# Partial sums and the residual added by accumulating transfers, PSUM copied by ACT

## The chip, the cores and the metric

The kernel runs on one core of a Trainium2 chip. A core has five engines that each work through their own instructions in order: PE (TensorE, matmuls, whose weight loads the profile lists as PEld), DVE (VectorE), ACT (ScalarE), POOL (GpSimd) and SP (SyncE, which here only starts transfers). They meet through semaphores. Matmuls write into PSUM, which DVE and ACT read; everything else lies in the core's buffer memory (SBUF) or in DRAM. Transfers (DMA) between DRAM and SBUF run beside the engines, on 16 DMA engines. The metric is the device time of one execution in microseconds (us). Before the change it is 1700.47 us, the median of three runs (1698.03 to 1700.65).

## The reference

One layer of a hybrid decoder for 2048 tokens of width 1024, in float32:

```python
h = rmsnorm(x, norm_pre)
proj = h @ w_in                       # 6416 columns, split into seven parts
y_ssd = ...                           # Mamba-2 scan of 16 heads, gated and normalised
y_sc = sc_b * causal_dwconv(sc_c * sc_h, sc_conv_w) * silu(z_sc)
mix = concatenate([y_ssd, y_sc]) @ w_out      # 2048 -> 1024
x = x + rmsnorm(mix, norm_post)               # the residual
gate = sigmoid(x @ w_ple_gate)                # 1024 -> 1024
return x + gate * (p @ w_ple_proj)
```

The change touches the second half of `mix`, its norm and the addition of the residual.

## The kernel before

All activations are held transposed: 128 of the 1024 features on the partitions, tokens along the free dimension. A tile is 128 x 512 float32, 256 KB; the 2048 tokens make four token groups (`tg` 0 to 3, `TG` = 512), the 1024 features eight blocks (`d` 0 to 7, `KD` = 8). Each float32 operand is split into a high part, a cast to the matmul's type, and the rest; a product takes three passes of matmuls (`PASSES`, function `mm3`). An output tile with eight input blocks thus takes 24 matmuls (line 214).

The program has four stages: the input projection with the convolutions (to about 1038 us), the scan of the heads, under which the half of `mix` that comes from `y_sc` is computed (tiles `os`, line 826, stored into DRAM as `part_d`), then the output projection's other half (`out_proj`, from about 1322 us), then the gate (`gate`, from about 1505 us).

In `out_proj` two token groups share the weights. A PSUM tile `mo` holds two output blocks, `d` and `d + 1`, of one group; three such tiles rotate (`pss`). For each block, in the order (group t, d), (t, d+1), (t+1, d), (t+1, d+1), PE does the 24 matmuls; then DVE adds the half in PSUM to the stored partial sum and writes the result as a tile of `x2` (line 1060), ACT squares it (lines 1062 and 1065), and DVE sums the squares into `ssq` (line 1066). `Loads` brings two blocks of `part_d`, 512 KB, per transfer into one of three buffers (line 769, on SP's queue). Below, the first block of a PSUM tile is its first half, the other its second half, and a unit is one block of one group: units 0 to 15 are groups 0 and 1, 16 to 31 groups 2 and 3, 32 to 63 the gate.

Other work is fixed to units by a table (`plan`): `mixes` prepares the operands `act_m` of a later group from loads `mraw` (lines 785, 203, 204); `norm` multiplies `ssq` with a matrix of 1/1024 on PE (`pn`, line 1072), takes the root on ACT and the reciprocal on DVE; `residual` scales `x2` on DVE (line 1081) and adds the input `x` to it (line 1082), loaded two blocks at a time as `xres` like `part`; `operands` makes the gate's operands `act_x2s` from it. Weights are loaded by SP, then cast by ACT (`ws_o`, line 138) and subtracted by DVE (line 139) into one of six slots.

The order in the source is not the order on the engines: a scheduler places the instructions of each engine by the times that it expects, within the dependencies, and every engine then runs its list in order. A waiting instruction holds up everything behind it on its engine, transfers on a queue too.

Of the kernel before, what the change touches and what calls it, by code (L numbers as in the profile page):

```python
# [7 lines left out]
F32 = mybir.dt.float32  # L8
F32R = mybir.dt.float32r
AF = mybir.ActivationFunctionType  # L10
ALU = mybir.AluOpType
# [4 lines left out]
P = 128  # L16
D = 1024
T = 2048
KD = D // P
KM = 2 * KD  # L20
TB = 1024
NB = T // TB
TG = 512
NG = T // TG
# [36 lines left out]
def hybrid_kernel(ctx: ExitStack, tc: tile.TileContext, xT, pT, w_t, w_dt, w_o, w_g, w_p, cols_d, cst_d, outT):  # L61
    nc = tc.nc
    V, S, G, TE = nc.vector, nc.scalar, nc.gpsimd, nc.tensor
# [7 lines left out]
    yz_d = [dram.tile([KD, P, TB], F32, name=f"yz_d{b}") for b in range(NB)]  # L71
# [4 lines left out]
    part_d = [dram.tile([KD, P, TG], F32, name=f"part_d{g}") for g in range(NG)]  # L76
    ysc_d = [dram.tile([KD, P, TB], F32, name=f"ysc_d{b}") for b in range(NB)]
# [262 lines left out]
    for b, prs, order in groups:  # L340
        src = lambda pr, i, jj, kk: w_t[tiles[pr][i], :, 4 * jj:4 * jj + 4, :]
# [20 lines left out]
    with ExitStack() as st:  # L362
# [352 lines left out]
        for b, prs, order in groups:  # L715
            to = {pr: takes(b, pr) for pr in prs}
            n = order_.index(prs)
# [28 lines left out]
    class Loads:  # L746
# [5 lines left out]
        def begin(self, kind, *at):  # L752
            if (kind, *at) in self.ready:
                return
            t = self.ready[(kind, *at)] = self.pool.tile([P, 2, TG], F32, tag="ld", name="_".join(map(str, (kind, *at))))
            if kind in ("mraw", "gn"):
                b, o = divmod(at[0] * TG, TB)
            if kind == "gn":
                src = grs_d[b][:, o:o + TG].partition_broadcast(P)
            else:  # L760
                if kind == "mraw":
                    k = at[1]
                    src = yz_d[b][k:k + 2, :, o:o + TG] if k < KD else ysc_d[b][k - KD:k - KD + 2, :, o:o + TG]
                elif kind == "part":
                    src = part_d[at[0]][at[1]:at[1] + 2]
                else:
                    src = xT[at[1]:at[1] + 2, :, at[0] * TG:(at[0] + 1) * TG]
                src = src.rearrange("k p t -> p k t")
            nc.sync.dma_start(t, src)

# [21 lines left out]
    def mm_bank(name):  # L792
        return psm.tile([P, TG], F32, tag="mm", name=name)
# [241 lines left out]

    with ExitStack() as st:
        pp = st.enter_context(tc.tile_pool(name="pp", bufs=2))
        L3 = Loads(st, "pl3", 3)

        x2s_, ssq_, rs_, sp_ = {}, {}, {}, {}  # L1040

        def out_proj(t):

            for tg in (t, t + 1):
                x2s_[tg] = [None] * KD
                ssq_[tg] = pp.tile([P, TG], F32, tag="ssq", name=f"ssq2_{tg}")
            for dp in range(0, KD, 2):
                sp = []
                for tg in (t, t + 1):
                    x2, ssq = x2s_[tg], ssq_[tg]  # L1050
                    ps = pss.tile([P, 2, TG], F32, tag="ssd", name=f"mo_{tg}_{dp}")
                    pt = L3.get("part", tg, dp)
                    for i in range(2):
                        for q in range(2):
                            if tg == t:
                                sp.append(W.next(len(sp)))
                            mm3([(ps[:, i, :], sp[2 * i + q], acts_o[tg])], 4 * q, 4, KD)
                        d = dp + i
                        x2[d] = pp.tile([P, TG], F32, tag="x2", name=f"x2_{tg}_{d}", bufs=NG * KD)
                        V.tensor_tensor(x2[d], ps[:, i, :], pt[:, i, :], ALU.add)  # L1060
                        if d == 0:
                            S.activation(ssq, x2[d], AF.Square)
                        else:
                            sq = pp.tile([P, TG], F32, tag="sq2", name=f"sq2_{tg}_{d}")
                            S.activation(sq, x2[d], AF.Square)
                            V.tensor_tensor(ssq, ssq, sq, ALU.add)
                        yield

        def norm(tg):

            ps = mm_bank(f"pn2_{tg}")
            TE.matmul(ps, ones_d, ssq_[tg], start=True, stop=True)
            rs = rs_[tg] = pp.tile([P, TG], F32, tag="rs2", name=f"rs2_{tg}")
            S.activation(rs, ps, AF.Sqrt, bias=epsc[:, 0:1])
            V.reciprocal(rs, rs)

        def residual(tg, d):

            x2, xk = x2s_[tg], L3.get("xres", tg, d)
            for i in range(2):  # L1080
                V.scalar_tensor_tensor(x2[d + i], x2[d + i], col(C_POST + d + i), rs_[tg], ALU.mult, ALU.mult)
                V.tensor_tensor(x2[d + i], x2[d + i], xk[:, i, :], ALU.add)

        def operands(tg, d):

# [27 lines left out]
        def after(unit, *steps):  # L1113
            plan.setdefault(unit, []).extend(steps)

        def second(tg, at_norm, at_res, at_ops):

            after(at_norm, lambda: norm(tg))
            for n, u in enumerate(at_res):
                after(u - 1, lambda d=2 * n: L3.begin("xres", tg, d))  # L1120
                after(u, lambda d=2 * n: residual(tg, d))
            for n, u in enumerate(at_ops):
                after(u, lambda d=2 * n: operands(tg, d))
# [15 lines left out]
        u = 0  # L1139
# [68 lines left out]
```

## Time and profile before

| What | Value |
|---|---|
| Median of three runs | 1700.47 us (1698.03 to 1700.65) |
| The profiled execution | 1696.41 us, its span 1694.7 us |
| Busy in the span | PE 98%, PEld 80%, DVE 74%, ACT 46%, POOL 3% |
| Chain that ended last | PE 85%, DMA 6%, DVE 6%, ACT 2%, issue 1% |
| Output projection, `mo` (line 214) | 768 matmuls, 180.9 us busy, 4.3 us idle before them |
| Gate, `mg` (line 214) | 768 matmuls, 176.8 us busy, 0.7 us idle before them |
| TensorE clock granted | 0.996 of full speed |

A row of a group reads: line, engine, operation, output and inputs with shapes, count, then busy time and the mean ns of one, then the idle time of the engine just before them and what ended it. In the rows of waits the engine and line on the left waited for what is on the right: us in total, times, longest. A row of the chain of waits or of the timeline begins with its start and its length in us. A row of windows holds the stretch, its length, the busy time of PE, PEld, DVE, ACT and POOL with their instructions, the granted clock, the DMA engines' busy share, and GB/s. A row of DMA issues ends with the count, the KB of one and the median us from issue to landing.

### The profile page before, as it was taken

The page shows a single profiled execution, that of the slowest core. Times are in us where ns is not written, and L with a number is a line of the kernel's source. Part 1 is how long each engine was busy: PE and PEld are TensorE (multiplying, and loading weights), DVE is VectorE, ACT ScalarE, POOL GpSimd, SP SyncE. Part 2 cuts the span into 40 slices and gives each one's busy share as a digit, 9 for nine tenths or more (in the row PEclk, how much of TensorE's full clock was granted, in tenths as well). Part 3 has the DMA queues.
Part 4 walks back from the last instruction along what each step waited for, and adds up shares of the span by engine and source line. Part 5 has one row for each costly group of instructions (what it writes and reads, how often), then busy time and mean ns, then how long its engine had stood idle before and what let it go on. Part 6 is the DMA issues. An engine that isn't in the chain of part 4 may idle for free.

```text
span 1694.7 us, 22635 instructions
## 1 busy us (share of the span) xinstructions
PE 1658.7 (98%) x8324; PEld 1351.9 (80%) x8324; DVE 1255.4 (74%) x1843; ACT 783.5 (46%) x1408; POOL 45.6 (3%) x79
## 2 busy tenths in 40 slices
PE   7999999999999999999999999999999899999998
PEld 5788888888888888888888888778777677788886
DVE  7997777988669867677777685689678748878632
ACT  7763444434337434343444353666575324252421
POOL 0000000000000100100000000000000000000000
PEclk9999999999999999999999999999999999999999
DMA  9462221773226322222222237789887735636422
GB/s 303 162 211 70 97 96 61 257 251 120 69 68 213 130 80 95 78 76 68 106 82 102 73 117 239 245 277 278 261 314 242 243 100 168 197 102 211 149 95 87
DMA packets 122691, 262.27 MB, mean 155 GB/s; under 512 B 17098, under 2 KB 19658, under 8 KB 121556
## 3 DMA queue, kind: packets, MB, share of 16 engines
q1 hardware_dynamic: 122580, 260.83, 46.4%
q8 instruction: 65, 1.06, 0.2%
q14 instruction: 46, 0.38, 0.1%
HBM read 192.45 MB, written 68.33 MB: 154 GB/s over the span
## 4 chain that ended last, share of the span: by engine, by line
PE 85%; DMA 6%; DVE 6%; ACT 2%; issue 1%; SPq 0%; DVEq 0%; ACTq 0%
PE mg L214 10%; PE mo L214 8%; PE os L826 6%; PE py L967 1%; PE A_xs1X L310 1%; PE A_gc6X L310 1%; PE A_gc7X L310 1%; PE A_gb6X L310 1%; PE A_z3X L310 1%; PE A_xs3X L310 1%; PE A_gc5X L310 1%; PE A_z2X L310 1%; PE A_xs2X L310 1%; PE A_gb4X L310 1%; PE A_gc4X L310 1%; PE A_gc3X L310 1%
## 5 line engine op out<-in xcount | busy, mean ns | idle before, releaser
L826 PE MATMUL os<-act_m,ws_os 128*128 128x512 f32 x768 | 186.0, 396 | 2.4 <-ACT po L830 1.7
L214 PE MATMUL mo<-act_m,ws_o 128*128 128x512 f32 x768 | 180.9, 396 | 4.3 <-DVE x L1060 4.3
L214 PEld LDWEIGHTS mo<-act_m,ws_o 128*128 128x128 f32 x768 | 144.1, 189 | 42.1 <-issue 6.1
L214 PE MATMUL mg<-act_x2s,ws_g 128*128 128x512 f32 x768 | 176.8, 391 | 0.7 <-ACT gth L1104 0.7
L826 PEld LDWEIGHTS os<-act_m,ws_os 128*128 128x128 f32 x768 | 141.2, 188 | 37.6 <-issue 6.6
L214 PEld LDWEIGHTS mg<-act_x2s,ws_g 128*128 128x128 f32 x768 | 143.0, 188 | 34.2 <-ACT gth L1104 4.4
L139 DVE TENSOR_TENSOR ws_A_gb<-wr_A_gb,ws_A_gb 128x512 fp32r<-128x512 f32 x96 | 65.8, 686 | 33.0 <-ACT ws_A_gb L138 32.9
L138 ACT CAST ws_A_gc<-wr_A_gc 128x512 fp32r<-128x512 f32 x96 | 59.7, 622 | 57.7 <-PE A_gc5X L310 8.3
L138 ACT CAST ws_A_gb<-wr_A_gb 128x512 fp32r<-128x512 f32 x96 | 59.7, 621 | 51.6 <-PE A_cb0Y L310 4.3
L604 DVE SCALAR_TENSOR_TENSOR xo<-ux,cols,xo 128x1024 f32<-128x1024 f32 x60 | 76.7, 1280 | 6.7 <-ACT xo L600 5.6
L939 ACT ACTIVATE m<-m,adt 128x128 f32<-128x128 f32 x256 | 77.5, 391 | 0.6 <-DMA m<-acs_d 0.5
L139 DVE TENSOR_TENSOR ws_A_gc<-wr_A_gc,ws_A_gc 128x512 fp32r<-128x512 f32 x96 | 66.0, 687 | 14.1 <-ACT ws_A_gc L138 12.8
L1105 DVE SCALAR_TENSOR_TENSOR gth<-gth,pe 128x512 f32<-128x512 f32 x32 | 22.1, 691 | 70.5 <-ACT gth L1104 70.4
L1104 ACT ACTIVATE gth<-mg 128x512 f32<-128x512 f32 x32 | 19.1, 598 | 103.7 <-PE mg L214 103.6
L214 PE MATMUL A_ple<-act_p,ws_p 128*128 128x512 f32 x192 | 48.2, 409 | 9.0 <-ACT ws_p L138 8.1
L942 DVE SCALAR_TENSOR_TENSOR m<-m,gsb 128x1024 f32<-128x1024 f32 x32 | 39.6, 1246 | 19.1 <-ACT m L939 16.8
L214 PEld LDWEIGHTS A_ple<-act_p,ws_p 128*128 128x128 f32 x192 | 37.4, 196 | 18.7 <-ACT ws_p L138 9.0
L139 DVE TENSOR_TENSOR ws_A_z<-wr_A_z,ws_A_z 128x512 fp32r<-128x512 f32 x48 | 32.9, 685 | 25.2 <-ACT ws_A_z L138 25.2
L203 ACT CAST act_m<-mraw 128x512 fp32r<-128x512 f32 x64 | 38.1, 621 | 28.9 <-DVE mraw L785 15.8
L138 ACT CAST ws_A_xs<-wr_A_xs 128x512 fp32r<-128x512 f32 x48 | 29.9, 623 | 44.3 <-issue 11.6
L138 ACT CAST ws_A_z<-wr_A_z 128x512 fp32r<-128x512 f32 x48 | 29.9, 623 | 41.9 <-DVE wr_A_z L187 8.6
L1060 DVE TENSOR_TENSOR x<-mo,part 128x512 f32<-128x512 f32 x32 | 22.0, 686 | 29.3 <-PE mo L214 29.3
(499 smaller groups left out, 3597.7 us busy)
## 6 DMA issues: line engine op xcount, KB each, us to landing
wr_A_gc<-in_w_t_dram SPq DMA_DIRECT2D x64, 256.0 KB, 2.5
wr_A_gb<-in_w_t_dram SPq DMA_DIRECT2D x64, 256.0 KB, 2.8
m<-acs_d SPq DMA_DIRECT2D x32, 512.0 KB, 7.7
ple_d<-A_pe SPq DMA_DIRECT2D x32, 256.0 KB, 5.1
wr_A_xs<-in_w_t_dram SPq DMA_DIRECT2D x32, 256.0 KB, 2.6
ysc_d<-vs SPq DMA_DIRECT2D x16, 512.0 KB, 2.7
wr_A_z<-in_w_t_dram SPq DMA_DIRECT2D x32, 256.0 KB, 3.0
xs_d<-xo SPq DMA_DIRECT2D x16, 512.0 KB, 4.0
```

The source lines that it names most:

```text
L138: S.copy(sp[:, 0, :kn, :], raw[:, :kn, :])
L139: V.tensor_tensor(sp[:, 1, :kn, :], raw[:, :kn, :], sp[:, 0, :kn, :].bitcast(F32), ALU.subtract)
L203: S.copy(a[:, 0, :], src)
L214: TE.matmul(out, sp[:, a, (k0 + k) % 4, :], act[k0 + k][:, b, :], start=k0 + k == 0 and q == 0, stop=k0 + k == n - 1 and q == 2)
L310: TE.matmul(out, sp[:, a, k % 4, :], t[:, b, ts_], start=p in OPENS and k == 0 and q == 0, stop=k == nk - 1 and q == 2, skip_group_check=True)
L604: V.scalar_tensor_tensor(o, u[:, q:q + TB], col(w0 + q), o, ALU.mult, ALU.add)
L826: TE.matmul(ps, sp[:, a, k, :], acts_o[tg][KD + kk][:, b_, :], start=kk == 0 and n == 0, stop=kk == KD - 1 and n == 2)
L939: S.activation(m[:, c, :], m[:, c, :], AF.Exp, bias=nacs[b][:, h, c:c + 1])
L942: V.scalar_tensor_tensor(mf, mf, 1.0, s["gsb"][gr], ALU.min, ALU.mult)
L1060: V.tensor_tensor(x2[d], ps[:, i, :], pt[:, i, :], ALU.add)
L1104: S.activation(th, ps, AF.Tanh, scale=0.5)
L1105: V.scalar_tensor_tensor(th, th, 1.0, pe, ALU.add, ALU.mult)
```

## The change

Four things are done in another way in `out_proj` and `residual`. The half in PSUM is copied by ACT into the tile of `x2`. The stored partial sum is added to it by a transfer from DRAM into that tile that accumulates, issued by POOL, 256 KB each. The residual is added in the same manner, after DVE's scaling. The squares and their sum are put off in the source by two units (`late`); what is left of them is done ahead of the last group's norm. The loads of `part` and `xres` with their three buffers go.

```diff
         def out_proj(t):
...
                     ps = pss.tile([P, 2, TG], F32, tag="ssd", name=f"mo_{tg}_{dp}")
-                    pt = L3.get("part", tg, dp)
                     for i in range(2):
...
                         x2[d] = pp.tile([P, TG], F32, tag="x2", name=f"x2_{tg}_{d}", bufs=NG * KD)
-                        V.tensor_tensor(x2[d], ps[:, i, :], pt[:, i, :], ALU.add)
-                        if d == 0:
-                            S.activation(ssq, x2[d], AF.Square)
-                        else:
-                            sq = pp.tile([P, TG], F32, tag="sq2", name=f"sq2_{tg}_{d}")
-                            S.activation(sq, x2[d], AF.Square)
-                            V.tensor_tensor(ssq, ssq, sq, ALU.add)
+                        S.copy(x2[d], ps[:, i, :])
+                        G.dma_start(x2[d], part_d[tg][d], accum_op=ALU.add)
+                        late.append(lambda tg=tg, d=d: squares(tg, d))
+                        if len(late) > 2:
+                            late.pop(0)()
                         yield
+        late = []
+        def squares(tg, d):
+            x2, ssq = x2s_[tg], ssq_[tg]
+            if d == 0:
+                S.activation(ssq, x2[d], AF.Square)
+            else:
+                sq = pp.tile([P, TG], F32, tag="sq2", name=f"sq2_{tg}_{d}")
+                S.activation(sq, x2[d], AF.Square)
+                V.tensor_tensor(ssq, ssq, sq, ALU.add)
         def norm(tg):
+            if tg == NG - 1:
+                while late:
+                    late.pop(0)()
...
         def residual(tg, d):
-            x2, xk = x2s_[tg], L3.get("xres", tg, d)
+            x2, ts_ = x2s_[tg], slice(tg * TG, (tg + 1) * TG)
             for i in range(2):
                 V.scalar_tensor_tensor(x2[d + i], x2[d + i], col(C_POST + d + i), rs_[tg], ALU.mult, ALU.mult)
-                V.tensor_tensor(x2[d + i], x2[d + i], xk[:, i, :], ALU.add)
+                G.dma_start(x2[d + i], xT[d + i, :, ts_], accum_op=ALU.add)
...
-                after(u - 1, lambda d=2 * n: L3.begin("xres", tg, d))
                 after(u, lambda d=2 * n: residual(tg, d))
```

The scheduler makes of it what follows. In the rows `x_0_4` is the tile of `x2` of group 0 and block 4, `mo_4` a PSUM tile of blocks 4 and 5, `sq` the squares, and the number behind a name tells buffers apart; square brackets name the engines or transfers whose semaphores the instruction waits for (DMAHW are SP's transfers, DMASW POOL's).

ACT in the middle of groups 0 and 1, blocks 2 to 4, before:

```order
L1065 ACTIVATE sq_0_2_11540<-x_0_2_11538 128x512 [waits DVE_49,Activation_49]
L1065 ACTIVATE sq_0_3_11569<-x_0_3_11567 128x512 [waits DVE_49,Activation_49]
L138 CAST ws_o_5_0_11636<-wr_o_5_0_11637 128x512 [waits PE_49]
L138 CAST ws_o_5_1_11641<-wr_o_5_1_11642 128x512 [waits PE_49]
L1065 ACTIVATE sq_1_2_11601<-x_1_2_11599 128x512 [waits DVE_49,Activation_49]
L138 CAST ws_o_6_0_11646<-wr_o_6_0_11647 128x512 [waits PE_49]
L138 CAST ws_o_6_1_11651<-wr_o_6_1_11652 128x512 [waits DMAHW6_49,PE_49]
L1065 ACTIVATE sq_1_3_11630<-x_1_3_11628 128x512 [waits DVE_49,Activation_49]
L1065 ACTIVATE sq_0_4_11682<-x_0_4_11680 128x512 [waits DVE_49,Activation_49]
```

and the same place now:

```order
L1053 COPY x_0_2_11529<-mo_2_11484 128x512 [waits PE_49]
L1068 ACTIVATE sq_0_2_11591<-x_0_2_11529 128x512 [waits DMASW4_49,DVE_49]
L1053 COPY x_0_3_11557<-mo_2_11484 128x512 [waits PE_49]
L138 CAST ws_o_5_0_11625<-wr_o_5_0_11626 128x512 [waits PE_49]
L1068 ACTIVATE sq_0_3_11621<-x_0_3_11557 128x512 [waits DMASW5_49,DVE_49]
L1053 COPY x_1_2_11588<-mo_2_11563 128x512 [waits PE_49]
L138 CAST ws_o_5_1_11630<-wr_o_5_1_11631 128x512
L1068 ACTIVATE sq_1_2_11672<-x_1_2_11588 128x512 [waits DMASW6_49,DVE_49]
L138 CAST ws_o_6_0_11635<-wr_o_6_0_11636 128x512 [waits PE_49]
L1053 COPY x_1_3_11618<-mo_2_11563 128x512 [waits PE_49]
L138 CAST ws_o_6_1_11640<-wr_o_6_1_11641 128x512 [waits DMAHW6_49]
L1068 ACTIVATE sq_1_3_11702<-x_1_3_11618 128x512 [waits DMASW7_49,DVE_49]
```

The copies have come in, and each square, which waits for POOL's transfer of its own tile, stands ahead of the copy of the next tile.

PE at the change from the first to the second half of the tile of group 0, blocks 4 and 5, before:

```order
L214 MATMUL mo_4_11633<-act_m_7_11249,ws_o_4_1_11509 128x512 x3
L214 MATMUL mo_4_11714<-act_m_0_11316,ws_o_4_0_11504 128x512 x3
L214 MATMUL mo_4_11714<-act_m_1_11320,ws_o_4_0_11504 128x512
L214 MATMUL mo_4_11633<-act_m_0_11181,ws_o_5_0_11636 128x512 [waits DVE_49,Activation_49]
L214 MATMUL mo_4_11633<-act_m_0_11181,ws_o_5_0_11636 128x512 x2
```

and now:

```order
L214 MATMUL mo_4_11624<-act_m_7_11249,ws_o_4_1_11500 128x512 x3
L214 MATMUL mo_4_11705<-act_m_0_11313,ws_o_4_0_11495 128x512 x3
L214 MATMUL mo_4_11705<-act_m_1_11317,ws_o_4_0_11495 128x512
L214 MATMUL mo_4_11624<-act_m_0_11181,ws_o_5_0_11625 128x512 [waits Activation_49]
L214 MATMUL mo_4_11624<-act_m_0_11181,ws_o_5_0_11625 128x512
```

The order is the same: the last matmuls of the first half, four of the other group's tile, then the second half, which waits until the first half has been taken out of PSUM, then by DVE's addition, now by ACT's copy.

POOL at the end of its list, before:

```order
L860 AFFINE_SELECT gsb_9848<-gsb_9848 128x1024 [waits DVE_49,Activation_49]
L919 COPY sprev_10421<-carry 128x128 [waits DVE_49,PE_49,Pool_49]
L919 COPY sprev_10724<-carry 128x128 [waits DVE_49,PE_49,Pool_49]
L919 COPY sprev_11027<-carry 128x128 [waits DVE_49,PE_49,Pool_49]
L1203 UNCONDITIONAL_BRANCH
```

Now 64 transfers follow the last copy of `sprev`; where groups 2 and 3 begin, they read:

```order
L1087 DMA x_0_5_11699<-in_xT_dram 128x512 [waits DMASW0_49,DVE_49]
L1054 DMA x_3_1_12138<-part_d_81 128x512 [waits DMASW1_49,Activation_49]
L1087 DMA x_0_6_11811<-in_xT_dram 128x512 [waits DMASW2_49,DVE_49]
L1087 DMA x_0_7_11847<-in_xT_dram 128x512 [waits DMASW3_49,DVE_49]
L1087 DMA x_1_0_11450<-in_xT_dram 128x512 [waits DMASW4_49,DVE_49]
L1087 DMA x_1_1_11478<-in_xT_dram 128x512 [waits DMASW5_49,DVE_49]
L1087 DMA x_1_2_11588<-in_xT_dram 128x512 [waits DMASW6_49,DVE_49]
L1054 DMA x_2_2_12193<-part_d_80 128x512 [waits DMASW7_49,Activation_49]
```

The residual's transfers of groups 0 and 1 (line 1087) stand between the partial sums of groups 2 and 3 (line 1054), in one queue.

More of the change, by code (lines that the diff above doesn't have):

```diff
@@ L755, in begin @@
             t = self.ready[(kind, *at)] = self.pool.tile([P, 2, TG], F32, tag="ld", name="_".join(map(str, (kind, *at))))
-            if kind in ("mraw", "gn"):
-                b, o = divmod(at[0] * TG, TB)
+            b, o = divmod(at[0] * TG, TB)
             if kind == "gn":
@@ L760, in begin @@
             else:
[L761 to L765, printed above, removed]
-                else:
-                    src = xT[at[1]:at[1] + 2, :, at[0] * TG:(at[0] + 1) * TG]
+                k = at[1]
+                src = yz_d[b][k:k + 2, :, o:o + TG] if k < KD else ysc_d[b][k - KD:k - KD + 2, :, o:o + TG]
                 src = src.rearrange("k p t -> p k t")
@@ L1037, in hybrid_kernel @@
         pp = st.enter_context(tc.tile_pool(name="pp", bufs=2))
-        L3 = Loads(st, "pl3", 3)
         x2s_, ssq_, rs_, sp_ = {}, {}, {}, {}
@@ L1049, in out_proj @@
                 for tg in (t, t + 1):
-                    x2, ssq = x2s_[tg], ssq_[tg]
+                    x2 = x2s_[tg]
                     ps = pss.tile([P, 2, TG], F32, tag="ssd", name=f"mo_{tg}_{dp}")
-                    pt = L3.get("part", tg, dp)
                     for i in range(2):
@@ L1059, in out_proj @@
                         x2[d] = pp.tile([P, TG], F32, tag="x2", name=f"x2_{tg}_{d}", bufs=NG * KD)
-                        V.tensor_tensor(x2[d], ps[:, i, :], pt[:, i, :], ALU.add)
-                        if d == 0:
-                            S.activation(ssq, x2[d], AF.Square)
-                        else:
-                            sq = pp.tile([P, TG], F32, tag="sq2", name=f"sq2_{tg}_{d}")
-                            S.activation(sq, x2[d], AF.Square)
-                            V.tensor_tensor(ssq, ssq, sq, ALU.add)
-                        yield
+                        S.copy(x2[d], ps[:, i, :])
[3 more added lines that the diff above has]
+                            late.pop(0)()
+                        yield
+        late = []
[7 more added lines that the diff above has]
+                V.tensor_tensor(ssq, ssq, sq, ALU.add)
         def norm(tg):
+            if tg == NG - 1:
+                while late:
+                    late.pop(0)()
             ps = mm_bank(f"pn2_{tg}")
```

## The prediction

> **What bounds the kernel now.** The row of engine busy times comes first, then a window over the output projection, from its first full tile to its end, then the waits of TensorE (PE) in that window.
>
> ```profile
> span 1694.7 us, 22635 instructions
> PE 1658.7 (98%) x8324; PEld 1351.9 (80%) x8324; DVE 1255.4 (74%) x1843; ACT 783.5 (46%) x1408; POOL 45.6 (3%) x79
> 1326.00:1516.00 190.00, 185.70 (x796) 148.60 (x793) 128.78 (x191) 68.10 (x110) 0.00 (x0) 0.99 0.49 158
> PE mo L214 <- DVE x L1060: 4.3, 4, 1.7
> ```
>
> PE is busy 185.70 of 190 us there (the columns are length, then busy time of PE, PE's weight loads, DVE, ACT, POOL, the granted clock, the DMA share and GB/s). All of its 4.3 us of idle time is four waits for DVE's line 1060, which empties a finished half of a PSUM tile. So 4.3 us is the most that a better way of emptying PSUM can give here. The chain of waits shows what made DVE late:
>
> ```profile
> 1348.76 6.03 DMA mraw<-yz_d
> 1357.49 0.61 DVE x L1060
> ...
> 1467.27 4.35 DMA xres<-in_xT_dram
> 1472.33 0.69 DVE x L1060
> 1473.02 0.14 issue
> 1473.15 6.85 PE mo L214 x29
> ...
> 1358.14 45.12 PE mo L214 x194
> ...
> 1460.00:1480.00 20.00, 18.39 (x81) 14.90 (x80) 13.76 (x22) 3.61 (x7) 0.00 (x0) 1.00 0.50 161
> ```
>
> DVE stood in its own queue behind an instruction whose load had not landed, and PE waited for the copy behind it; the last row, a window of 20 us, has 1.61 us of PE's idle time around the second of these. The chain's piece of 194 matmuls gives PE's undisturbed pace: 45.12/194 = 0.2326 us a matmul, so 5.58 us for the 24 of one output tile. That pace is reached when somebody empties each half on time.
>
> **How much time there is to empty a half.** PE does the tiles in an interleaved order: after the first half of a pair it does four matmuls of the other token group, 4 x 0.2326 = 0.93 us, and then wants the second half of the same pair, whose first matmul waits until the first half is copied out (the order rows above show that wait, before and after). So the copy of each first half must be done 0.93 us after its last matmul. ACT's timeline shows when halves are finished, since its squares follow DVE's line 1060 at once:
>
> ```profile
> 1375.59 0.63 ACT L1065 ACTIVATE sq<-x 128x512 f32<-128x512 f32 x1 [0.16 <-DVE x L1060]
> 1380.12 0.63 ACT L1065 ACTIVATE sq<-x 128x512 f32<-128x512 f32 x1 [3.90 <-DVE x L1060]
> 1386.68 0.63 ACT L1065 ACTIVATE sq<-x 128x512 f32<-128x512 f32 x1 [5.93 <-DVE x L1060]
> 1391.21 0.63 ACT L1065 ACTIVATE sq<-x 128x512 f32<-128x512 f32 x1 [0.16 <-DVE x L1060]
> ```
>
> The steps are 4.53, 6.56 and 4.53 us: long inside a pair, short from a second half to the next first half, 11.09 us for two tiles. The tight copy, that of a first half, comes at the end of the short step.
>
> **The change, part by part.** *Removed from DVE:* 32 additions of line 1060 and 32 of line 1082, and from SP 32 loads of 512 KB (the stored partial sums and the residual).
>
> ```profile
> L1060 DVE TENSOR_TENSOR x<-mo,part 128x512 f32<-128x512 f32 x32 | 22.0, 686 | 29.3 <-PE mo L214 29.3
> L1082 DVE TENSOR_TENSOR x<-x,xres 128x512 f32<-128x512 f32 x32 | 21.3, 683 | 5.6 <-DMA xres<-in_xT_dram 5.5
> L830 ACT COPY po<-os 128x512 f32<-128x512 f32 x8 | 4.6, 579 | 4.7 <-PE os L826 4.7
> L1065 ACT ACTIVATE sq<-x 128x512 f32<-128x512 f32 x28 | 17.7, 633 | 49.5 <-DVE x L1060 49.4
> ```
>
> That is 43.3 us of DVE, which idles 190 - 128.8 = 61 us in the window anyway: it buys nothing but the stalls. The stall behind xres (1.6 us) goes. Those behind mraw do not go surely, because ACT's casts of act_m wait for the same loads through DVE, and the PSUM copies now stand behind those casts. I take 2 of the 4.3 us as gained.
>
> *Added to ACT:* 32 copies of PSUM, priced by line 830, which copies the same shape from PSUM: 0.579 us each, 18.5 us beside 122 us of idle time. The sum of ACT's work costs nothing; its order may. The source says that squares follow two tiles later, but the order on ACT has each square ahead of the very next tile's copy. So ACT copies a half, then waits in its square for that half's accumulating transfer, and cannot copy the next half before. Call L the time from the end of a copy until its transfer has landed. A first half's copy is in time if copy + L + square + copy fit into the short step and PE's cover: 0.58 + L + 0.63 + 0.58 <= 4.53 + 0.93, so L <= 3.67 us, less two hand-overs of 0.16 us (the idle time in the rows above): **L <= 3.35 us**. Above it PE stalls by L - 3.35 in each of the 16 pairs. Above about 4.8 us ACT has no rest on the long step either: a copy, its transfer and its square then take 1.21 + 0.32 + L per tile, and a pair takes 2 x (1.53 + L) instead of 11.09.
>
> *Added to POOL's queue:* 64 accumulating transfers. The trace of before has none (POOL's busy time in the window is 0.00), so L has no row. The nearest:
>
> ```profile
> part<-part_d SPq DMA_DIRECT2D x16, 512.0 KB, 5.8
> xres<-in_xT_dram SPq DMA_DIRECT2D x11, 512.0 KB, 4.2
> mraw<-yz_d SPq DMA_DIRECT2D x10, 512.0 KB, 7.0
> wr_o<-in_w_o_dram SPq DMA_DIRECT2D x19, 256.0 KB, 3.5
> DMA to landing us min/median/max: 2.5/2.8/3.8
> ```
>
> The first four are the median landings of plain loads in this very window, the last those of the 256 KB loads of ple_d in the gate stage, where less is in flight. An accumulating transfer takes 256 KB from DRAM and must get at as many bytes of the buffer, so it lies between a plain load of 256 KB (2.5 us at the lowest, 3.5 in this stage) and one of 512 KB (4.2 to 7.0). Both ends: 2.5 us costs nothing, 5.8 us costs 16 x (2 x 7.33 - 11.09) = 57 us. I take 4.6 us, a little over the xres row: the same residual rows by size, and another engine's queue to go through. That costs 16 x (4.6 - 3.35) = **20 us**.
>
> [...]
>
> *The residual's transfers in the same queue.* POOL issues in order, and 16 residual transfers of the first two groups stand among the partial sums of units 17 to 23: three ahead of x_3_0, three ahead of x_3_1, five ahead of x_2_2, five ahead of x_2_3. They become ready as fast as DVE's line 1081 makes them:
>
> ```profile
> L1081 DVE SCALAR_TENSOR_TENSOR x<-x,cols,rs 128x512 f32<-128x512 f32 x32 | 22.7, 744 | 0.0
> GB/s 303 162 211 70 97 96 61 257 251 120 69 68 213 130 80 95 78 76 68 106 82 102 73 117 239 245 277 278 261 314 242 243 100 168 197 102 211 149 95 87
> ```
>
> One each 0.74 us, while a transfer that touches 512 KB needs 1.67 us at the page's highest rate, 314 GB/s. Five ahead are up to 8.3 us of delay, three up to 5. Bounds: 0, if they have drained, and 27 us for all four. I take **8 us**. For the other groups the residual is added in the gate stage, five tiles or more (28 us) ahead of its casts, and the norm's matmul comes 68 matmuls, 16 us, after the last tile that it needs: both covered, as long as ACT lags no more than some microseconds. Without that cover the norm's matmul would pay ACT's lag once per group.
>
> *Sum:* -2 + 20 + 8 = +26 us. The profiled execution took 1696.4 us (span 1694.7), so 1722; it lies 4 us under the median of the runs, 1700.5, and against that the forecast is **1726 us**.
>
> **The rivals.** (1) *The cover holds:* transfers land within 3.35 us, ACT is never late, and DVE's stalls go. For it: the 2.5 to 2.8 us loads of 256 KB. Against it: 3.5 us in this stage. It gives the whole 4.3 us, 1696.2. [...] (2) *A draw:* L about 3.4 to 3.5, stalls of 2 us in all, and one more of 2 to 3 us in the residual's crowd: 1700 to 1703. (3) *ACT is the pace:* landings like mraw's 7.0 us: 16 x (2 x 8.53 - 11.09) = 96 us and 8 for the crowd: 1800. For it: 49% of the DMA engines' time is taken in the window already; against it: each transfer has half of mraw's bytes from DRAM. It decides from L = 4.8 on.
>
> **How the numbers follow.** The forecast (from L = 3.7 without a crowd, +4 us, to L = 5.8 with a crowd of 13, +68) has 0.62 and spans 1704 to 1768; rival 1 has 0.13, rival 2 0.12, rival 3 0.13. The range 1697 to 1768 leaves out about one in ten on each side. 0.2% (3.4 us) is about what a measurement can tell from no change: faster 0.12, same 0.13, slower 0.75.
>
> **What would show it.** In the changed profile: squares (now line 1065 or 1068) waiting for a DMA, about L each, less 0.6 where a cast stands ahead, and PE's matmuls of mo waiting for ACT's copy once per pair, by about 1.2 us, and more at x_2_2 and x_2_3. The mg matmuls and the stretch ahead of 1320 us should stay. Landings of the accumulating transfers under 3.4 us, or copies that stay on time behind waiting squares, would make the forecast wrong; so would waits of DVE or of the norm's matmul that exceed those of the copies.

## The result and the profile after

The changed kernel takes 1750.45 us (median of 4 runs, 1748.77 to 1755.48) against 1700.33 us for the kernel before on the same chip: a ratio of 1.031, with a 95% interval of 1.0288 to 1.0333. It is slower by 50 us; the forecast was 26. The profiled execution has a span of 1749.5 us, 54.8 us more than the 1694.7 of before, and all sums below are made against these two spans.

The page of the changed kernel first: engines, then the groups of matmuls of the output projection and the gate, the last group of the scan, and the squares.

```profile
span 1749.5 us, 22704 instructions
PE 1672.0 (96%) x8324; PEld 1359.4 (78%) x8324; DVE 1216.6 (70%) x1779; ACT 796.3 (46%) x1440; POOL 101.7 (6%) x143
...
L214 PE MATMUL mo<-act_m,ws_o 128*128 128x512 f32 x768 | 190.1, 408 | 40.5 <-ACT x L1053 40.2
...
L820 PE MATMUL os<-act_m,ws_os 128*128 128x512 f32 x768 | 187.6, 398 | 4.4 <-ACT po L824 3.7
...
L214 PE MATMUL mg<-act_x2s,ws_g 128*128 128x512 f32 x768 | 178.5, 394 | 4.2 <-ACT gth L1109 4.2
...
L1068 ACT ACTIVATE sq<-x 128x512 f32<-128x512 f32 x28 | 17.7, 631 | 117.1 <-DMA x<-part_d 117.1
```

DVE lost 39 us of work, as meant. PE waits 40.5 us ahead of the matmuls of `mo` where it had waited 4.3, 40.2 of it for ACT's copy (line 1053), and ACT in turn waits 117 us in its squares for POOL's transfers. One number is easy to pass over: the same 768 matmuls of `mo` are *busy* for 190.1 us instead of 180.9.

The chain of waits (start, length, what) shows one turn of the loop:

```profile
1350.85 0.48 ACT x L1053
1351.33 0.28 issue
1351.61 4.63 DMA x<-part_d
1356.24 0.02 issue
1356.27 0.63 ACT ssq L1065
1356.90 0.51 ACT ws_o L138
1357.41 0.49 ACT x L1053
```

A copy ends at 1351.33, its transfer lands at 1356.24, 4.91 us later; only then come the square, a cast and the next copy. PE's timeline in the same stage gives the stalls with their lengths in the brackets (start, length, engine and line, operation, count):

```profile
1351.37 11.22 PE L214 MATMUL mo<-act_m,ws_o 128*128 128x512 f32 x48 [2.52 <-ACT x L1053]
1364.50 11.18 PE L214 MATMUL mo<-act_m,ws_o 128*128 128x512 f32 x48 [1.91 <-ACT x L1053]
1376.53 11.20 PE L214 MATMUL mo<-act_m,ws_o 128*128 128x512 f32 x48 [0.85 <-ACT x L1053]
1390.46 12.78 PE L214 MATMUL mo<-act_m,ws_o 128*128 128x512 f32 x48 [2.73 <-ACT x L1053]
...
1447.85 12.81 PE L214 MATMUL mo<-act_m,ws_o 128*128 128x512 f32 x48 [3.99 <-ACT x L1053]
...
1479.69 12.55 PE L214 MATMUL mo<-act_m,ws_o 128*128 128x512 f32 x48 [6.10 <-ACT x L1053]
1502.10 13.23 PE L214 MATMUL mo<-act_m,ws_o 128*128 128x512 f32 x48 [9.87 <-ACT x L1053]
...
1571.70 8.53 PE L214 MATMUL mg<-act_x2s,ws_g 128*128 128x512 f32 x30 [3.53 <-ACT gth L1109]
```

There are two things in these rows. First the brackets: eleven ordinary stalls of 0.85 to 2.93 us (20.3 us in all), one of 3.99 and two of 6.10 and 9.87. Then the lengths: 48 matmuls take 11.2 us at full pace, but 12.6 to 13.2 behind the longer stalls. The windows show the reason (columns: the stretch, its length, busy time of PE, PE's weight loads, DVE, ACT and POOL, then the granted clock):

```profile
1385.00:1390.00 5.00, 2.73 (x13) 1.92 (x11) 0.04 (x1) 0.70 (x2) 0.00 (x0) 1.00 0.55 123
1390.00:1395.00 5.00, 4.54 (x13) 3.65 (x14) 0.65 (x1) 0.40 (x1) 0.88 (x1) 0.66 0.34 52
1395.00:1400.00 5.00, 5.00 (x24) 4.13 (x23) 0.69 (x1) 1.57 (x3) 0.86 (x1) 1.00 0.00 0
...
1500.00:1505.00 5.00, 2.90 (x7) 2.33 (x8) 1.39 (x2) 1.62 (x3) 0.88 (x1) 0.50 0.23 20
```

Behind the stall of 2.73 us the granted clock is 0.66 in a window of 5 us, so TensorE ran at half clock for some 3.4 us of it (1 - 0.34 = 0.66, and 0.34 x 5 / 0.5 = 3.4; the trace's clock record has 0.50 for 3.41 us from 1390.49 us on), and during and after the longest stall it is 0.50. The 48 matmuls of that row take 12.78 us instead of 11.2, 1.6 more. The stall is paid a second time, in part.

Put together, against before:

| Where the 54.8 us came from | us |
|---|---|
| eleven ordinary stalls of `mo` | +20.3 |
| the two stalls behind the residual's transfers (6.10, 9.87) | +16.0 |
| the stall at the casts of `act_m` (3.99) | +4.0 |
| half clock behind six stalls (the excess of the rows over 0.2326 us a matmul) | +9.9 |
| waits of the gate's matmuls, 4.2 instead of 0.7 | +3.5 |
| DVE's four old stalls, gone | -4.3 |
| the scan's group `os`, 3.6 longer, and 1.8 without a place | +5.4 |

That `os` is longer is mostly not the change's: in five kernels below that run at the time of before it is 187.2 to 187.7 us busy too, instead of the 186.0 of that one profile of before. Its waits, 4.4 us now, were 2.4 before and are 0.8 to 3.1 in those five. The 1.8 us stay unexplained.

### The profile page after: what moved, and what is told of

Its sections match the earlier page's. It is cut to its first block, busy times and chain, and to the rows that moved or that the text cites. A ratio compares the mean times of both kernels' runs of the same rounds, so it can differ in the third digit from the quotient of the medians.

```text
span 1749.5 us, 22704 instructions
## 1 busy us (share of the span) xinstructions
PE 1672.0 (96%) x8324; PEld 1359.4 (78%) x8324; DVE 1216.6 (70%) x1779; ACT 796.3 (46%) x1440; POOL 101.7 (6%) x143
## 4 chain that ended last, share of the span: by engine, by line
PE 74%; issue 9%; DMA 7%; DVE 5%; ACT 2%; POOL 2%; SPq 0%; POOLq 0%; ACTq 0%; DVEq 0%
PE mg L214 10%; PE os L820 6%; DMA x<-part_d 2%; PE A_xs1X L310 1%; DMA yz_d<-xs 1%; PE A_gc6X L310 1%; PE A_gc7X L310 1%; PE A_gb6X L310 1%; PE A_z3X L310 1%; PE A_xs3X L310 1%; PE A_gc5X L310 1%; PE A_z2X L310 1%; PE A_xs2X L310 1%; PE A_gc4X L310 1%; PE A_z1X L310 1%
## 5 line engine op out<-in xcount | busy, mean ns | idle before, releaser
L214 PE MATMUL mo<-act_m,ws_o 128*128 128x512 f32 x768 | 190.1, 408 | 40.5 <-ACT x L1053 40.2
L214 PEld LDWEIGHTS mo<-act_m,ws_o 128*128 128x128 f32 x768 | 149.8, 197 | 82.9 <-ACT x L1053 47.4
L1069 DVE TENSOR_TENSOR ssq<-ssq,sq 128x512 f32<-128x512 f32 x28 | 19.4, 692 | 106.7 <-ACT sq L1068 106.7
L1068 ACT ACTIVATE sq<-x 128x512 f32<-128x512 f32 x28 | 17.7, 631 | 117.1 <-DMA x<-part_d 117.1
```

What stands on the lines that cost most here:

```text
L214: TE.matmul(out, sp[:, a, (k0 + k) % 4, :], act[k0 + k][:, b, :], start=k0 + k == 0 and q == 0, stop=k0 + k == n - 1 and q == 2)
```

## Experiments: is it the place of the squares, the queue, or the transfers themselves?

The theory so far: nothing that was added is too slow by itself. ACT's in-order list makes the next copy wait for a transfer that the copy doesn't need (theory A). The rival: 64 accumulating transfers, or POOL's handling of them, cost the time wherever the squares stand (B). Four kernels separate them; the kernel before took 1697.62 us beside them.

**Squares where the source has them.** A dependence without a semaphore puts each square on ACT behind the copy of the tile two units later. Everything else, the copies and the 64 transfers too, stays.

```diff
-                        S.copy(x2[d], ps[:, i, :])
+                        cp = S.copy(x2[d], ps[:, i, :])
...
-                        late.append(lambda tg=tg, d=d: squares(tg, d))
+                        late.append(lambda cp=None, tg=tg, d=d: squares(tg, d, cp))
                         if len(late) > 2:
-                            late.pop(0)()
+                            late.pop(0)(cp)
...
+            act = S.activation(sq, x2[d], AF.Square)
+            if cp is not None:
+                tc.add_manual_dep(act.ins, cp.ins.name, NOSYNC, reason="square behind a later copy")
```

> The changed kernel with each square put on ACT behind the copy of the tile two units later, as its source reads; transfers, copies and POOL's queue stay. Theory A (a square that waits for its own transfer holds up the next copy, and the clock falls because PE stops): PE's waits for the copies fall from 40.2 us to under 5, the granted clock returns to 0.99 or more in the output projection, 1700 us, between 1695 and 1706. Rival B (the accumulating transfers cost by themselves, by their traffic or by POOL's queue): above 1735. Between 1710 and 1735: the residual's crowd is longer than two tiles cover.

Measured: 1709.39 us, ratio 1.0073 (1.0046 to 1.0101). Some 40 of the 50 us are gone (by the ratios, 1.0310 and 1.0073), with every transfer still there; rival B falls. Theory A's own range was missed: PE still waits 9.7 us for the copies, not under 5. Most of the rest has one place, again from PE's timeline and from the page (of the longest of the six runs, 1717.17 us):

```profile
1444.64 34.05 PE L214 MATMUL mo<-act_m,ws_o 128*128 128x512 f32 x148
1487.37 35.02 PE L214 MATMUL mo<-act_m,ws_o 128*128 128x512 f32 x140 [8.68 <-ACT x L1053]
...
L214 PE MATMUL mo<-act_m,ws_o 128*128 128x512 f32 x768 | 184.0, 401 | 9.9 <-ACT x L1053 9.7
```

One stall of 8.68 us, where the residual's transfers of groups 0 and 1 stand in the queue. Two tiles of delay do not cover that; that is the mechanism of the expectation's third case (1710 to 1735, the crowd is longer than two tiles cover), though the time lies just under its range.

**The residual by SP and DVE as before,** the squares as in the changed kernel:

```diff
-                G.dma_start(x2[d + i], xT[d + i, :, ts_], accum_op=ALU.add)
+                V.tensor_tensor(x2[d + i], x2[d + i], xk[:, i, :], ALU.add)
...
+                after(u - 1, lambda d=2 * n: L3.begin("xres", tg, d))
```

> The changed kernel with the residual loaded by SP and added by DVE as before; the partial sums stay accumulating. Theory A (16 us or so of the loss are residual transfers ahead of the partial sums in POOL's queue): the three waits of 4.0, 6.1 and 9.9 us become ordinary ones of 1 to 2.5, ACT's longest wait for a transfer falls from 10.4 to under 6, 1728 us, between 1720 and 1736. Rival (the stage is short of DMA bandwidth, the queue does not matter): above 1742.

Measured: 1745.32 us, ratio 1.0289 (1.0252 to 1.0327). That is a miss: 5 us under the changed kernel and not 22, and by the ratios not even surely different from it. By the time alone the rival (bandwidth, the queue does not matter) would have won. PE's timeline says otherwise:

```profile
1448.54 13.16 PE L214 MATMUL mo<-act_m,ws_o 128*128 128x512 f32 x48 [5.05 <-ACT x L1060]
1476.62 12.78 PE L214 MATMUL mo<-act_m,ws_o 128*128 128x512 f32 x48 [1.98 <-ACT x L1060]
1492.20 11.22 PE L214 MATMUL mo<-act_m,ws_o 128*128 128x512 f32 x48 [2.80 <-ACT x L1060]
1507.72 12.61 PE L214 MATMUL mo<-act_m,ws_o 128*128 128x512 f32 x48 [4.31 <-ACT x L1060]
```

The 6.10 and 9.87 us became 1.98 and 2.80, as theory A has it. But the stall at 1448 is there as before (5.05 for 3.99), so it never was the queue's. There a copy stands behind two casts of `act_m`, which wait 0.91 us for DVE's scaling of `mraw`; DVE comes to it only after it has summed the late square. The copy's transfer, issued beside a load of 512 KB of `mraw`, then takes 6.2 us to land (6.1 in the changed kernel). And a new stall of 4.31 us came, where a square still waits for its transfer: from 1465 to 1506 us, with seven loads of `xres` by SP, the partial sums land in 6.0 us (median). ACT's longest wait for a transfer is 6.9 us, not under 6. So this run does not tell the queue from the traffic; the spread transfers below do. In an order in which every square can hold up a copy, the wait that is removed lets the next one show: all waits of `mo` fell by 8.2 us only (40.5 to 32.3), and the half clock stayed (192.1 us busy).

**The partial sums by SP and DVE as before,** only the residual accumulating:

```diff
+                    pt = L3.get("part", tg, dp)
...
-                        S.copy(x2[d], ps[:, i, :])
-                        G.dma_start(x2[d], part_d[tg][d], accum_op=ALU.add)
+                        V.tensor_tensor(x2[d], ps[:, i, :], pt[:, i, :], ALU.add)
```

> The changed kernel with the partial sums loaded by SP and added by DVE from PSUM as before; only the residual is accumulated by POOL. Theory A (all of the loss goes through squares that wait for transfers): no engine waits for a transfer ahead of a PSUM copy but for the loads of mraw and part, 1700 us, between 1696 and 1705. Rival (the residual's transfers cost by themselves, in the gate stage or by traffic): above 1712.

Measured: 1697.26 us, ratio 1.0007 (0.9988 to 1.0025): the time of before, as expected. The residual's 32 accumulating transfers cost nothing that can be measured when no partial sum stands behind them.

**Both: squares behind, residual by SP.**

> Squares behind the copy two units later, and the residual by SP and DVE: the partial sums alone are accumulated. Theory A: no wait of PE for a copy over 1 us, 1698 us, between 1694 and 1703, within 3 us of the kernel with the squares behind alone, or below it by what the crowd still costs there. Rival B (the accumulating transfers cost by themselves): above 1715.

Measured: 1697.49 us, ratio 0.9994 (0.9977 to 1.0011).

```profile
L214 PE MATMUL mo<-act_m,ws_o 128*128 128x512 f32 x768 | 178.4, 393 | 1.8 <-ACT x L1060 1.6
```

The 32 copies on ACT and the 32 accumulating partial sums are all there, and PE waits 1.8 us ahead of `mo` (one wait of 1.6 us, where none over 1 was expected). This half of the change costs nothing and also brings nothing that can be measured; nor does the other half, by the run before. What cost 50 us is the order.

## Experiments: the crowd and the price of the accumulation

**The residual's transfers spread.** Squares behind, as in the kernel of 1709.4 us; in POOL's queue the residual's transfers now stand two at a time behind a partial sum, over units 18 to 27.

```diff
-                        G.dma_start(x2[d], part_d[tg][d], accum_op=ALU.add)
+                        sent[0] = G.dma_start(x2[d], part_d[tg][d], accum_op=ALU.add)
...
-                G.dma_start(x2[d + i], xT[d + i, :, ts_], accum_op=ALU.add)
+                r = G.dma_start(x2[d + i], xT[d + i, :, ts_], accum_op=ALU.add)
+                tc.add_manual_dep(r.ins, sent[0].ins.name, NOSYNC, reason="residual behind a partial sum")
...
-        second(0, 16, (19, 20, 21, 22), (29, 29, 30, 30))
-        second(1, 18, (24, 25, 26, 27), (31, 31, 32, 32))
+        second(0, 16, (18, 19, 20, 22), (29, 29, 30, 30))
+        second(1, 18, (23, 24, 26, 27), (31, 31, 32, 32))
```

> Squares behind, as in the kernel of 1709.4 us; the residual's transfers of groups 0 and 1 stay accumulating and in POOL's queue, but at most two stand between two partial sums, spread over units 18 to 27, instead of three, three, five and five in units 17 to 23. Theory F (what is left over 1697 is the burst: accumulating transfers take the DMA engines 1.6 us each and the partial sums stand behind them): the stall of 8.7 us goes, mo waits under 3 us, 1699 us, between 1696 and 1703. Rival (the residual's transfers cost by their traffic, wherever they stand): above 1706.

Measured: 1698.75 us, ratio 1.0016 (1.0000 to 1.0032); waits of `mo` 2.8 us in all. The whole change, squares and queue in the right order, is within 0.3% of before. The same 64 transfers, the same bytes, another order in one queue: 10 us less (ratios of 1.0073 and 1.0016). So the crowd is a matter of place, and 10 us is its price with the squares out of the way.

What each transfer takes is read from the DMA queues of the kernel with the squares behind, in the stretch from 1440 to 1490 us (packets, MB, share of 16 engines' time), q0 being POOL's and q1 SP's:

```profile
q0 software_dynamic: 3326, 6.06, 74.9%
q1 hardware_dynamic: 1116, 2.04, 12.4%
```

6.06 MB took 0.749 x 50 = 37.5 us of all 16 engines, so 256 KB take 1.62 us; SP's plain loads take 0.80 us for as much. The prediction had 1.67 us.

**The same crowd with the squares still in the way:** the changed kernel with the residual spread in the same manner.

> The changed kernel, its squares still ahead of the next copy, with the residual's transfers of groups 0 and 1 spread over units 18 to 27, at most two between two partial sums. Theory F (the stalls of 6.1 and 9.9 us are the burst in POOL's queue): they become ordinary ones of 1 to 3 us, but with one or two residual transfers ahead of most partial sums of these units, whose waits grow by a part of 1.6 us; 1738 us, between 1731 and 1744. Rival (the traffic of the residual costs the same wherever it stands): 1748 or more.

Measured: 1741.10 us, ratio 1.0269 (1.0237 to 1.0302), within the expected range, some 7 us under the changed kernel by the ratios, whose intervals still overlap. The stalls show it better than the time: the two became 1.22 and 1.51 us, while that at the casts of `act_m` grew to 7.12 (the transfer there took 7.1 us to land) and two later ones to 3.18 and 3.15.

**Without the add.** The changed kernel with `accum_op` taken out of both kinds of transfer. The partial sum and the residual then replace what is in the tile, so both additions are left out of the result; queue, order, sizes and waits are the same.

```diff
-                        G.dma_start(x2[d], part_d[tg][d], accum_op=ALU.add)
+                        G.dma_start(x2[d], part_d[tg][d])
...
-                G.dma_start(x2[d + i], xT[d + i, :, ts_], accum_op=ALU.add)
+                G.dma_start(x2[d + i], xT[d + i, :, ts_])
```

> The changed kernel with every transfer of POOL as a plain copy instead of an accumulating one; queue, order, sizes and waits are the same. The stored partial sum and the residual replace what is in the tile: both additions are left out. It prices the accumulation in L. Theory G (the add doubles what a transfer takes of the DMA engines): landings of 3.2 us in the median instead of 4.3, PE's waits for copies under 12 us instead of 40, most of them in pairs where casts stand in ACT's way, crowd waits under 3 us each, 1708 us, between 1700 and 1718. Rival H (L is POOL's way of issuing, not the add): landings stay at 4 us or more, 1735 or more.

Measured: 1705.62 us, ratio 1.0044 (1.0027 to 1.0060). The partial sums' landings from 1330 to 1570 us, and the queue's share of the 16 engines from 1440 to 1490, both of this kernel:

```profile
x<-part_d POOLq DMA_DIRECT2D x32, 256.0 KB, 3.0
...
q0 software_dynamic: 1920, 6.29, 40.4%
```

and the landings of the changed kernel in the same stretch:

```profile
x<-part_d POOLq DMA_DIRECT2D x32, 256.0 KB, 4.3
```

A plain transfer of 256 KB from POOL lands here in 3.0 us, an accumulating one in the changed kernel in 4.3 (medians); of the engines' time it takes 0.404 x 50 / 6.29 x 0.262 = 0.84 us, and 1.62 with the add. So theory G holds: the add, not the queue it is issued on, lengthened the wait; up to 0.33 of the 1.3 us may lie in POOL's own instruction, which takes 0.54 us for a plain transfer and 0.87 for an accumulating one. With 3.0 us and the 0.3 that pass from the end of a copy to the start of its transfer, L is 3.3: just at the limit of 3.35 that the prediction had worked out, and PE's waits ahead of `mo` fall to 10.6 us, 3.56 of them at the casts of `act_m`.

## Experiments: what halves the clock

The busy time of `mo` had not been in the forecast at all. Theory C: PE is granted half the clock for a stretch once it has stood still for some 2 us (in the rows above the stall of 1.98 us has 48 matmuls in 12.78 us behind it, that of 1.91 us 48 in 11.18; but that of 2.80 has 48 in 11.22). Rival D: the sum of the stalls decides. Rival E: the accumulating transfers' traffic does. To tell them apart, stalls were put into the kernel that runs at the time of before (squares behind, residual by SP) without touching a transfer: ACT copies a first half several times instead of once.

```diff
+                        for _ in range(2 if i == 0 else 0):
+                            S.copy(x2[d], ps[:, i, :])
                         cp = S.copy(x2[d], ps[:, i, :])
```

and, in the other kernel, seven further copies in 5 of the 16 pairs.

> Squares behind and the residual by SP, as in the kernel that runs at the time of before (1697.5 us); added: ACT copies each first half of a pair three times instead of once, so that PE waits some 1.0 to 1.6 us for it in each of the 16 pairs. No transfer is changed. It puts some 16 x 1.3 = 21 us of stalls into PE without anything that waits for a transfer. Theory C (the granted clock halves for a stretch only behind a stall of about 2 us or more): matmuls of mo stay under 182 us busy, the clock at 0.99 or more, 1718 us, between 1712 and 1725. Rival D (the clock falls with the sum of the stalls): mo at 188 to 191 us busy, 1728. Rival E (the clock falls through the accumulating transfers' traffic): as theory C here.

> The same base; added: ACT copies the first half eight times instead of once in 5 of the 16 pairs alone, so that PE waits about 4 us in each: 5 x 4.1 = 20 us of stalls, the same sum as with many short ones. Theory C: each of the five is followed by a stretch at half clock that costs 1.6 us, mo busy 8 us more than the base's 178.4, so 186 to 188, 1726 us, between 1720 and 1732, and some 8 us over the kernel with many short stalls for the same idle time. Rival D (the sum decides): both kernels show the same busy time of mo. Rival E (traffic of accumulating transfers): mo stays under 182, 1718.

Measured: 1699.07 us (ratio 1.0001, 0.9985 to 1.0018) and 1700.17 us (1.0015, 0.9999 to 1.0030). Both missed, since PE hardly stalled (0.4 and 2.5 us ahead of `mo`). The scheduler knows what a copy on ACT takes, and moved PE's list. The matmuls of one stretch in the two programs:

```
tile, half: matmuls     base                    seven more copies
mo_4 first half                20                      17
mo_4' (next group) first half   4                      23
mo_4 second half               24                      24
```

With a longer copy it put 23 matmuls instead of 4 between the two halves. The other side of this is the changed kernel itself, whose list has 4 there: the scheduler put each square, with a transfer of 4.3 us ahead of it, directly in front of a copy for which PE waits 0.93 us later.

So the two were run again with PE's order held: no more than four matmuls of a later tile may go ahead of a second half.

```diff
+                            ms = mm3([(ps[:, i, :], sp[2 * i + q], acts_o[tg])], 4 * q, 4, KD)
+                            if q == 0 and i:
+                                half2 = ms[0]
+                            elif q == 0 and half2 is not None:
+                                tc.add_manual_dep(ms[4].ins, half2.ins.name, NOSYNC, reason="no more than four ahead")
```

> As the kernel with three copies of each first half (squares behind, residual by SP), but PE's order is held: no more than four matmuls of a later tile may stand between a first half and its second half, as in the changed kernel, where the scheduler had put up to 23 there once it knew that ACT takes longer. So now PE does wait: 16 stalls of 1.0 to 2.0 us, some 21 us in all. Theory C (the clock halves for a stretch only behind a stall of about 2 us or more): mo busy under 183 us, 1718 us, between 1712 and 1726. Rival D (the sum of the stalls decides): mo busy 188 to 191, 1728. Rival E (accumulating transfers' traffic slows the clock): as C.

> As the kernel with eight copies in 5 pairs, with PE's order held in the same way: five stalls of 3.3 to 4.7 us, some 20 us in all, with the transfers as they were. Theory C: each is followed by a stretch at half clock that costs 1.6 us, mo busy 186 to 188, 1726 us, between 1720 and 1732. Rival D: mo busy as in the kernel with many short stalls. Rival E: mo stays under 182, 1717.

Measured: 1714.09 us (ratio 1.0097, 1.0069 to 1.0125) and 1728.25 us (1.0183, 1.0158 to 1.0209), both in theory C's ranges. `mo` is busy 184.9 and 186.4 us, against the base's 178.4: the first is above what C expected (under 183) and below what D did (188 to 191), and the waits of `mo` (17.2 and 23.2 us) were meant to be equal and are not, so the groups decide nothing. The rows decide. Many short stalls:

```profile
1372.61 11.18 PE L215 MATMUL mo<-act_m,ws_o 128*128 128x512 f32 x48 [1.39 <-ACT x L1069]
1384.80 11.17 PE L215 MATMUL mo<-act_m,ws_o 128*128 128x512 f32 x48 [1.01 <-ACT x L1069]
...
1511.50 11.87 PE L215 MATMUL mo<-act_m,ws_o 128*128 128x512 f32 x44 [1.91 <-ACT x L1069]
```

and few long ones:

```profile
1362.08 23.74 PE L215 MATMUL mo<-act_m,ws_o 128*128 128x512 f32 x96 [3.87 <-ACT x L1069]
1389.92 22.82 PE L215 MATMUL mo<-act_m,ws_o 128*128 128x512 f32 x92 [4.10 <-ACT x L1069]
1417.73 12.74 PE L215 MATMUL mo<-act_m,ws_o 128*128 128x512 f32 x48 [5.00 <-ACT x L1069]
...
1473.87 22.12 PE L215 MATMUL mo<-act_m,ws_o 128*128 128x512 f32 x96 [3.19 <-ACT x L1069]
```

At 0.2326 us a matmul, 44, 48, 92 and 96 take 10.2, 11.2, 21.4 and 22.3 us. The stalls up to 1.39 us leave the pace as it is, one after the other; that of 1.91 costs 1.6 us more, and those of 3.87, 4.10 and 5.00 cost 1.4 to 1.6 each. That of 3.19 cost nothing more, so length alone does not decide, and theory C is too simple. These stalls come from copies on ACT, with the transfers as they were in a kernel whose granted clock was 0.996 in the mean (here 0.994 and 0.990): rivals D and E fall.

All stalls of `mo` and `mg` that the timelines of the thirteen profiles show from 1325 to 1620 us, with the row behind them at least 17 matmuls long, sorted by length. A row counts as slowed where it took over 0.9 us more than 0.2326 us a matmul:

```
stall           rows    slowed
under 1.8 us      64         1   (it came right behind another stall of 2.0 us)
1.8 to 3.0 us     20        12
3.0 to 9.9 us     17        15
```

What sets them apart is in the clock records of the traces. The stretches at half clock in these stages last 3.41 us or two or three times that (3.41, 6.83 and 10.24 in the changed kernel), and within a profile their starts lie whole multiples of 3.41 us apart. In the changed kernel they start at 1325.64, 1390.49, 1431.45, 1448.52, 1475.83, 1496.31 and 1571.40 us, which are steps of 19, 12, 5, 8, 6 and 22 times 3.413 us: a grid that the stalls between them did not shift. The windows of two stalls, cut on this grid, show the difference, first that of 1.91 us ahead of 1511.50 in the kernel with many short stalls, then that of 3.19 ahead of 1473.87 in the other:

```profile
1509.58:1513.00 3.42, 1.51 (x8) 1.24 (x8) 0.69 (x1) 2.79 (x5) 0.86 (x1) 1.00 0.18 67
1513.00:1516.41 3.41, 3.41 (x10) 2.65 (x9) 2.08 (x3) 1.97 (x4) 0.00 (x0) 0.50 0.54 77
...
1468.92:1472.33 3.41, 1.76 (x8) 1.13 (x6) 3.41 (x7) 3.25 (x6) 0.00 (x0) 1.00 0.86 274
1472.33:1475.74 3.41, 1.87 (x8) 1.57 (x9) 3.41 (x7) 1.96 (x4) 0.86 (x1) 1.00 0.63 219
```

The first stall lies in one window, 1.91 of its 3.42 us idle, and the next window runs at 0.50. The second is cut into 1.65 and 1.54 us, and the clock stays at 1.00. Of the 101 stalls, 28 left PE idle for 1.84 us or more of one window, and 27 of these rows are slowed; of the other 73 only the one behind another stall is. This was read from the profiles afterwards; no run moved a stall on the grid to test it.

## Why the prediction was wrong in size

Its direction, its reason and its range held (1704 to 1768 for the forecast's case); the size, 26 us for 50, did not. Two of its steps failed: the residual's crowd, taken at 8 us, cost 16.0, and the lost clock, 9.9 us, was put at nothing. By its own steps:

- **PE bounds the kernel, and a copy that comes late is the price.** Right. All 40.2 us of new waits of `mo` are for line 1053, and moving the squares alone takes away some 40 of the 50 us.
- **L = 4.6 us, limit 3.35 us.** Right on both sides. The median landing is 4.3 us, 0.3 after the copy; and without the add, where L is 3.3, most stalls went (10.6 us of waits ahead of `mo` for 40.5).
- **16 x 1.25 = 20 us.** That the sum is right (20.3) is in part luck: it was eleven stalls of 1.84 us in the mean, not sixteen of 1.25. Two of the other pairs fell into the crowd, one stands at the casts, and two show no stall.
- **-2 us for DVE's stalls.** All 4.3 went, but 4.0 came back at the casts of `act_m`. The prediction named that place ("the PSUM copies now stand behind those casts") and gave it no price of its own. Not quite its reason: the casts waited 0.92 us for DVE, which stood behind the sum of a late square and not behind a load, and the transfer then landed in 6.1 us. Net -0.3.
- **8 us for the residual's crowd.** This is the term of the sum that failed in size: 16.0 us in the changed kernel, or 13.5 over the two ordinary stalls of 1.25 us that the 20 us already hold. Its working had the mechanism and the rate (1.67 us a transfer, measured 1.62), gave bounds of 0 to 27, and then took a value at a third of the upper one. ACT's rows of the crowd show why it was too low:

```profile
1470.34 0.63 ACT L1065 ACTIVATE ssq<-x 128x512 f32<-128x512 f32 x1 [5.15 <-DMA x<-part_d]
1470.87 0.57 ACT L1053 COPY x<-mo 128x512 f32<-128x512 f32 x1
1478.53 0.63 ACT L1068 ACTIVATE sq<-x 128x512 f32<-128x512 f32 x1 [6.57 <-DMA x<-part_d]
1479.07 0.57 ACT L1053 COPY x<-mo 128x512 f32<-128x512 f32 x1
1488.88 0.63 ACT L1068 ACTIVATE sq<-x 128x512 f32<-128x512 f32 x1 [9.25 <-DMA x<-part_d]
1489.42 0.57 ACT L1053 COPY x<-mo 128x512 f32<-128x512 f32 x1
1500.95 0.63 ACT L1068 ACTIVATE sq<-x 128x512 f32<-128x512 f32 x1 [10.44 <-DMA x<-part_d]
```

  Four squares in a row wait 5.15, 6.57, 9.25 and 10.44 us. The prediction's own rule says that above L = 4.8 nothing is left to absorb a delay: a pair then takes 2 x (1.53 + L), and each further microsecond of landing goes in full to PE, in both tiles. The other 28 squares wait 4.0 us in the median; over that these four are late by 1.2, 2.6, 5.3 and 6.4, together some 15, near the 16.0 that PE lost. By that rule the delays of a crowd add up. Taking a third of their sum was a guess that the prediction's own rule did not support.
- **The residuals of the gate stage and the norm's matmul are covered.** True for those two, but a square of the last tiles stands ahead of the gate's first tanh on ACT: PE waits 3.53 us at 1571.70, and the clock is 0.50 for 3.41 us from 1571.40 on. Missed, 3.5 us.
- **What has no step: the clock.** 9.9 us. The prediction summed idle time and took 0.2326 us for every matmul outside it; it had no term for matmuls that run slower behind a stall. The records show the half clock, in windows of 3.41 us on the grid above, behind 27 of the 28 stalls in which PE stood still for 1.84 us or more of one window: here a little over half a window without work was enough.

Of the rivals, the cover that holds (1696) fell with landings of 4.3 us; the kernel without the add, at 1705.62, comes within 10 us of it. The draw fell. ACT as the pace with L = 7 (1800) came true for four tiles only, the crowd's. That the scheduler had undone "two tiles later" was seen and is what the forecast rests on; what that order costs as a whole, some 40 us, was not priced.

## What to carry to other kernels

A delayed use in the source is not a delay on the engine: look where the scheduler put the instruction that waits for the transfer, and what stands behind it, and if need be tie it behind the instruction it must not hold up (1750 to 1709 us here, and to 1699 with the queue's order mended as well). Where a path has lost its slack, price a burst by its sum and not by a share of its bound: four squares late by some 15 us together went with 16.0 us of PE's time here. And look behind the longer stalls of TensorE for lost clock, which shows as longer busy time: behind 27 of the 37 stalls over 1.8 us it was 1.2 to 2.9 us here, 1.6 in the median.

## What the runs showed of the hardware that was not expected

- An accumulating transfer of 256 KB took 1.62 us of the 16 DMA engines (squares behind, 1440 to 1490 us), a plain one on the same queue 0.84 (without the add), and SP's 0.80 (squares behind); it landed in 4.3 us (changed kernel) instead of 3.0 (without the add), both medians.
- The granted clock fell to 0.50 for 3.41 us or two or three times that, from starts that lie whole multiples of 3.41 us apart within a profile. The rows were slowed behind 15 of 17 stalls over 3 us, behind 12 of 20 from 1.8 to 3 us, and behind no stall of less that stood by itself; whether PE stood still for 1.84 us or more within one window told the slowed rows from the others in all but two of the 101.
- In the crowd POOL sends 13 transfers between 1460.3 and 1485.5 us, in the kernel with the squares behind: one in some 1.9 us, though issuing one takes it 0.87 and the DMA engines do one in 1.62. Its timeline names nothing that it waited for ahead of most of them:

```profile
1476.48 0.86 POOL L1087 DMA_DIRECT2D x<-in_xT_dram  x1 [0.96 <-issue]
1481.62 0.89 POOL L1054 DMA_DIRECT2D x<-part_d  x1 [4.27 <-issue]
```

  What held it 4.27 us ahead of the partial sum at 1481.62 stays open.
